# A running logsumexp over 4096 rows: Exp and Ln by column chunks, a carry in two halves, and loads and stores on one queue

## The chip, the cores and the metric

The kernel runs on one core of a Trainium2 chip. A core has a matrix engine (TensorE, PE in the profile, with PEld for its weight loads), a vector engine (VectorE, DVE), an engine for functions such as exp and ln (ScalarE, ACT), a general one (GpSimd, POOL) and one that mostly issues transfers (SyncE, SP). Each engine takes its instructions in order. 16 DMA engines move data between the large memory (HBM) and the on-chip memory (SBUF); PE writes its results to a separate accumulation memory (PSUM).

The metric is device time in microseconds (us), the median over several runs. The times before the change are 1268.48 to 1272.39 us over 8 runs, median 1270.67 us.

## The reference

The input x has the shape (4, 4096, 4128) in float32: 4 batches, 4096 rows that are scanned in order, 4128 independent columns. The output is the running logsumexp along the rows:

```
out[:, 0, :] = x[:, 0, :]
for t in range(1, S):
    mx = maximum(out[:, t-1, :], x[:, t, :])
    out[:, t, :] = mx + log(exp(out[:, t-1, :] - mx) + exp(x[:, t, :] - mx))
```

So out[t] = ln(exp(x[0]) + ... + exp(x[t])). The kernel computes it in that form, without the maximum: Exp of everything, a running sum, Ln of the sums.

## The kernel before, in words

The rows are cut into steps of 256 (P * R = 128 x 2), so there are 4 x 16 = 64 steps, and the running sum passes from each step to the next within a batch. A step's tile `xt` is 128 partitions by 2 rows by 4128 columns of float32: partition p holds the rows 2p and 2p+1 of the step, which lie next to each other in HBM, so that one partition's part is one piece of 33024 bytes. One load (L135) and one store (L126) move the whole tile, 4128 KB each. `xt` has 5 buffers; the results are written back into the same buffer and stored from it, so a buffer is free for another load only when its store has landed.

Exp of the whole tile is one instruction (L139), into a float16 tile `et`. The running sum over the 256 rows is made by matrix products with constant 128 x 128 matrices, in column chunks of 1024 (`CH`), each as two matmuls of 512 (`MM`); every matmul goes through the helper at L80. For the first of the two rows of each partition, `head(c)` adds in one PSUM tile `pt`:

- `incl` times the first rows: all first rows up to and with this partition;
- `excl` times the second rows: all second rows of the partitions before;
- `last` times `carry[c]`: the sum at the end of the step before (left out at the first step of a batch).

Ln (L98) turns that into the output of the first rows. Then `second(c)` adds `ident` times the second rows onto the same PSUM tile, Ln (L105) gives the second rows, and DVE copies the whole PSUM tile to `carry[c]` in float16 (L106). `last` has ones in its last row only, so the next step takes partition 127 of the carry, which holds the total. There are four chunks of 1024 and a tail of 32 columns, which has its own small PSUM tile `qt`, one Ln (L124) and one copy (L125). `pt` has 3 buffers, each of 1024 float32 columns.

The order is written out by hand (`manual_schedule`), and the engines follow it. The loop at L133 issues, for step i+1, the load and Exp, and then the scan of step i: on ACT, Exp of step i+1 stands ahead of all Ln of step i. Loads are on SP's queue. Stores are on GpSimd's (L126), which does nothing else after the constants are built. So two DMA queues feed the same 16 DMA engines: q1 with the loads, q0 with the stores.

Of the kernel before, what the change touches and what calls it, by code (L numbers as in the profile page):

```python
# [1 line left out]

# [4 lines left out]

FP32 = mybir.dt.float32
FP16 = mybir.dt.float16
ACT = mybir.ActivationFunctionType  # L10
P = 128
R = 2
CH = 1024
MM = 512


def _constants(nc, pool):


    def tri(base, name):  # L20
        t = pool.tile([P, P], FP16, name=name)
        nc.gpsimd.memset(t, 1.0)

        nc.gpsimd.affine_select(  # L24
            out=t, in_=t, pattern=[[1, P]], compare_op=mybir.AluOpType.is_ge,
            fill=0.0, base=base, channel_multiplier=-1,
        )
        return t

    def ones_where_zero(base, mult, step, name):  # L30
        t = pool.tile([P, P], FP16, name=name)
        nc.gpsimd.memset(t, 0.0)
        nc.gpsimd.affine_select(  # L33
            out=t, in_=t, pattern=[[step, P]], compare_op=mybir.AluOpType.not_equal,
            fill=1.0, base=base, channel_multiplier=mult,
        )
        return t

    return (
        tri(0, "incl"),  # L40
        tri(-1, "excl"),
        ones_where_zero(0, 1, -1, "ident"),
        ones_where_zero(-(P - 1), 1, 0, "last"),
    )


@with_exitstack
def kernel(
    ctx: ExitStack,
    tc: tile.TileContext,  # L50
    x: bass.AP,
    out: bass.AP,
):

    nc = tc.nc
    B, S, D = x.shape
    rows = P * R
    n_t = S // rows  # L60
    assert S % rows == 0
    n_main = D // CH
    tail = D - n_main * CH
    t0 = n_main * CH

    nc.scalar.preload_act_table_set("natural_log_exp_and_others")  # L66
    consts = ctx.enter_context(tc.tile_pool(name="consts", bufs=1))
    incl, excl, ident, last = _constants(nc, consts)

    xpool = ctx.enter_context(tc.tile_pool(name="xpool", bufs=5))  # L70
    epool = ctx.enter_context(tc.tile_pool(name="epool", bufs=2))
    cpool = ctx.enter_context(tc.tile_pool(name="cpool", bufs=1))
    pmain = ctx.enter_context(tc.tile_pool(name="pmain", bufs=3, space=bass.MemoryType.PSUM))
    ptail = ctx.enter_context(tc.tile_pool(name="ptail", bufs=2, space=bass.MemoryType.PSUM))

    carry = [cpool.tile([P, CH], FP16, name=f"carry{c}") for c in range(n_main)]
    carry_t = cpool.tile([P, tail], FP16, name="carry_t") if tail else None

    def mm(pt, w, rhs, start, stop):
        nc.tensor.matmul(pt, lhsT=w, rhs=rhs, start=start, stop=stop, skip_group_check=True)  # L80

    def scan(b, k, xt, et):
        first = k == 0

        def head(c):
            pt = pmain.tile([P, CH], FP32, name="pt")
            for s in range(0, CH, MM):
                o = pt[:, s:s + MM]
                seg = slice(c * CH + s, c * CH + s + MM)
                mm(o, incl, et[:, 0, seg], True, False)  # L90
            for s in range(0, CH, MM):
                o = pt[:, s:s + MM]
                seg = slice(c * CH + s, c * CH + s + MM)
                mm(o, excl, et[:, 1, seg], False, first)
            if not first:
                for s in range(0, CH, MM):
                    mm(pt[:, s:s + MM], last, carry[c][:, s:s + MM], False, True)
            nc.scalar.activation(xt[:, 0, c * CH:(c + 1) * CH], pt, ACT.Ln)  # L98
            return pt

        def second(c, pt):
            for s in range(0, CH, MM):
                seg = slice(c * CH + s, c * CH + s + MM)
                mm(pt[:, s:s + MM], ident, et[:, 1, seg], False, True)
            nc.scalar.activation(xt[:, 1, c * CH:(c + 1) * CH], pt, ACT.Ln)  # L105
            nc.vector.tensor_copy(carry[c], pt)  # L106

        prev = None
        for c in range(n_main):
            pt = head(c)  # L110
            if prev is not None:
                second(c - 1, prev)
            prev = pt
        if tail:
            qt = ptail.tile([P, R, tail], FP32, name="qt")
            seg = slice(t0, D)
            for j in range(R):
                mm(qt[:, j, :], incl, et[:, 0, seg], j == 0, False)
                mm(qt[:, j, :], incl if j else excl, et[:, 1, seg], False, first)
                if not first:  # L120
                    mm(qt[:, j, :], last, carry_t, False, True)
        second(n_main - 1, prev)
        if tail:
            nc.scalar.activation(xt[:, :, t0:D], qt, ACT.Ln)  # L124
            nc.vector.tensor_copy(carry_t, qt[:, 1, :])  # L125
        nc.gpsimd.dma_start(  # L126
            out=out[b, k * rows:(k + 1) * rows, :].rearrange("(p j) d -> p j d", j=R), in_=xt,
        )

    ctx.enter_context(tc.manual_schedule())  # L130
    work = [(b, k) for b in range(B) for k in range(n_t)]
    pending = None
    for b, k in work:  # L133
        xt = xpool.tile([P, R, D], FP32, name="xt")
        nc.sync.dma_start(  # L135
            out=xt, in_=x[b, k * rows:(k + 1) * rows, :].rearrange("(p j) d -> p j d", j=R),
        )
        et = epool.tile([P, R, D], FP16, name="et")
        nc.scalar.activation(et, xt, ACT.Exp)  # L139
        if pending is not None:  # L140
            scan(*pending)
        pending = (b, k, xt, et)
    scan(*pending)


# [1 line left out]
_INS = ['x']  # L147
_OUTS = [((4, 4096, 4128), 'float32')]


# [23 lines left out]
```

## Time and profile before

| what | value |
|---|---|
| median of 8 runs | 1270.67 us |
| the profiled execution's own time | 1270.67 us |
| its span | 1269.0 us |
| PE busy | 611.2 us, 48% |
| DVE busy | 313.8 us, 25% |
| ACT busy | 948.9 us, 75% |
| Exp (L139), 64 instructions | 453.4 us, 7084 ns each |
| Ln (L98 and L105), 512 instructions | 254.2 and 255.0 us, 1019 and 1027 ns each |
| carry copy (L106), 256 instructions | 307.6 us, 1222 ns each |
| mean granted clock of PE | 0.761 |
| read from HBM, written to HBM | 270.53 MB, 270.53 MB |
| mean rate over the span | 426 GB/s |

Busy time of an engine is the time in which it works on at least one instruction, so neighbours that overlap a little are not counted twice. The profile cuts the span in 40 equal slices of 31.7 us; a row of digits gives an engine's busy share in each in tenths, and the rows DMA and GB/s give the mean busy share of the 16 DMA engines and what they moved. In a list of waits, each line names who waited, the instruction it waited for, the total in us, how many times, and the longest. In a table of stretches, each line has the stretch, its length, and for each engine its busy time and instructions, then the granted clock of PE, the DMA share and the rate; a packet's bytes are counted where it starts, so a share or a rate can pass the limit a little in a short stretch.

### The profile page before, as it was taken

Reading aid. Unit: us, or ns where it says so; the run is one execution under the profiler, and the core shown is the slowest. Engines: PE = TensorE matmul, PEld = TensorE weight load, DVE = VectorE, ACT = ScalarE, POOL = GpSimd, SP = SyncE. Lnnn points to the kernel's source line nnn. Section 1 sums busy time; section 2 is a strip of 40 time slices with the busy share of each in tenths; the row PEclk is TensorE's granted clock in tenths of the full one; section 3 lists DMA queues with packets and bytes.
Section 4 is the critical chain, followed back from the end, with each engine's and each line's share of the span. In section 5 each row is a group of like instructions: output and inputs, shape, how many; then the busy total and the mean of one; then the engine's idle time right before and its main releaser. Section 6 shows DMA issues by size and latency. Waiting matters only on the chain.

```text
span 1269.0 us, 6438 instructions
## 1 busy us (share of the span) xinstructions
PE 611.2 (48%) x2392; PEld 242.6 (19%) x2392; DVE 313.8 (25%) x320; ACT 948.9 (75%) x641; POOL 36.0 (3%) x76
## 2 busy tenths in 40 slices
PE   1565355354454454544535445454453554544543
PEld 0222122121121221211212112121121221211211
DVE  0332122231231222312223122132231222312213
ACT  5887777777777777677776777777777777677774
POOL 0000000000000000000000000000000000000000
PEclk9787787786777867778768687786877877768777
DMA  9999999999999999999999999999999999999996
GB/s 401 424 420 433 434 433 434 432 433 433 432 433 432 432 433 433 433 433 433 433 433 433 433 432 433 433 433 433 432 433 433 433 432 433 432 434 433 433 407 271
DMA packets 18463, 541.47 MB, mean 427 GB/s; under 512 B 2048, under 2 KB 2048, under 8 KB 2048
## 3 DMA queue, kind: packets, MB, share of 16 engines
q1 hardware_dynamic: 9216, 270.54, 49.6%
q0 software_dynamic: 9216, 270.54, 49.5%
q8 instruction: 18, 0.29, 0.1%
q14 instruction: 13, 0.11, 0.0%
HBM read 270.53 MB, written 270.53 MB: 426 GB/s over the span
## 4 chain that ended last, share of the span: by engine, by line
issue 89%; DMA 6%; POOL 2%; ACT 1%; PE 0%; DVE 0%; POOLq 0%; DVEq 0%; SPq 0%
DMA xt<-in_x_dram 3%; DMA out_dram<-xt 3%; POOL out_dram L126 2%; PE pt L80 0%; ACT xt L98 0%; ACT xt L105 0%; DVE carry L106 0%; POOLq L126 0%; DVEq L169 0%; DVE carry_t L125 0%; ACT et L139 0%; SPq L135 0%; DVEq L125 0%
## 5 line engine op out<-in xcount | busy, mean ns | idle before, releaser
L139 ACT ACTIVATE et<-xt 128x8256 f16<-128x8256 f32 x64 | 453.4, 7084 | 178.5 <-DMA xt<-in_x_dram 178.5
L106 DVE CAST carry<-pt 128x1024 f16<-128x1024 f32 x256 | 307.6, 1222 | 940.9 <-ACT xt L105 940.9
L80 PE MATMUL pt<-et,ident 128*128 128x512 f16 x512 | 198.9, 479 | 599.8 <-ACT xt L98 599.8
L98 ACT ACTIVATE xt<-pt 128x1024 f32<-128x1024 f32 x256 | 254.2, 1019 | 113.4 <-PE pt L80 112.7
L105 ACT ACTIVATE xt<-pt 128x1024 f32<-128x1024 f32 x256 | 255.0, 1027 | 11.7 <-PE pt L80 11.7
L80 PE MATMUL pt<-et,incl 128*128 128x512 f16 x512 | 194.2, 468 | 40.9 <-DVE carry L106 20.5
L80 PE MATMUL pt<-et,excl 128*128 128x512 f16 x512 | 187.5, 454 | 0.0
L80 PEld LDWEIGHTS <-ident 128*128 128x128 f16 x512 | 56.0, 109 | 680.2 <-issue 656.8
L80 PE MATMUL pt<-carry,last 128*128 128x512 f16 x480 | 167.5, 436 | 0.0
L80 PEld LDWEIGHTS <-incl 128*128 128x128 f16 x704 | 74.2, 112 | 153.2 <-issue 116.6
L80 PEld LDWEIGHTS <-excl 128*128 128x128 f16 x576 | 65.0, 113 | 97.5 <-issue 51.6
L80 PEld LDWEIGHTS <-last 128*128 128x128 f16 x600 | 63.6, 108 | 78.0 <-issue 37.2
L126 POOL DMA_DIRECT2D out_dram<-xt x64 | 34.2, 534 | 1217.4 <-ACT xt L124 1217.4
L80 PE MATMUL qt<-et,incl 128*128 128x32 f16 x192 | 17.9, 178 | 0.0
L124 ACT ACTIVATE xt<-qt 128x64 f32<-128x64 f32 x64 | 16.2, 253 | 0.0
L80 PE MATMUL qt<-carry_t,last 128*128 128x32 f16 x120 | 15.1, 176 | 0.0
L125 DVE CAST carry_t<-qt 128x32 f16<-128x32 f32 x64 | 11.6, 181 | 0.0
L80 PE MATMUL qt<-et,excl 128*128 128x32 f16 x64 | 11.3, 177 | 0.0
L66 ACT ACT_TABLE_LOAD x1 | 1.3, 1283 | 0.8 <-PEq L158 0.8
L24 POOL TENSOR_SCALAR_AFFINE_SELECT incl<-incl 128x128 f16<-128x128 f16 x1 | 0.3, 287 | 0.0
L24 POOL TENSOR_SCALAR_AFFINE_SELECT excl<-excl 128x128 f16<-128x128 f16 x1 | 0.3, 286 | 0.0
L33 POOL TENSOR_SCALAR_AFFINE_SELECT ident<-ident 128x128 f16<-128x128 f16 x1 | 0.3, 286 | 0.0
(9 smaller groups left out, 1.5 us busy)
## 6 DMA issues: line engine op xcount, KB each, us to landing
xt<-in_x_dram SPq DMA_DIRECT2D x64, 4128.0 KB, 27.0
out_dram<-xt POOLq DMA_DIRECT2D x64, 4128.0 KB, 34.2
```

Source lines behind the costliest of these rows:

```text
L24: nc.gpsimd.affine_select(out=t, in_=t, pattern=[[1, P]], compare_op=mybir.AluOpType.is_ge, fill=0.0, base=base, channel_multiplier=-1,)
L33: nc.gpsimd.affine_select(out=t, in_=t, pattern=[[step, P]], compare_op=mybir.AluOpType.not_equal, fill=1.0, base=base, channel_multiplier ...
L66: nc.scalar.preload_act_table_set("natural_log_exp_and_others")
L80: nc.tensor.matmul(pt, lhsT=w, rhs=rhs, start=start, stop=stop, skip_group_check=True)
L98: nc.scalar.activation(xt[:, 0, c * CH:(c + 1) * CH], pt, ACT.Ln)
L105: nc.scalar.activation(xt[:, 1, c * CH:(c + 1) * CH], pt, ACT.Ln)
L106: nc.vector.tensor_copy(carry[c], pt)
L124: nc.scalar.activation(xt[:, :, t0:D], qt, ACT.Ln)
L125: nc.vector.tensor_copy(carry_t, qt[:, 1, :])
L126: nc.gpsimd.dma_start(out=out[b, k * rows:(k + 1) * rows, :].rearrange("(p j) d -> p j d", j=R), in_=xt,)
L139: nc.scalar.activation(et, xt, ACT.Exp)
```

## The change

The matrices stay, and so do the bytes moved, the buffers of `xt` (5) and of PSUM (3 and 2). What changes:

- Exp is done by column chunk: three instructions of 2 x 1024 and one of 2 x 1056 elements per partition, each into its own `et` tile (4 buffers of one chunk in place of 2 of a whole step). The tail's columns are in the last chunk's tile.
- A step is no longer spread over two turns of the loop. Within a step, ACT's order is Exp 0, Exp 1, Ln of chunk 0's first rows, Exp 2, Ln of chunk 1's first rows, Ln of chunk 0's second rows, Exp 3, and so on. PE's order is written so that `head(c)` and, for the last chunk, the tail's matmuls stand ahead of `second(c-1)`.
- The carry is kept in two halves. DVE copies partitions 96 to 127 of PSUM to float16 (`HI`), and writes the difference between PSUM and that copy to partitions 32 to 63 (`LO`). `pick` replaces `last`, with ones in the rows 127 and 63, so that the matmul adds the rounded total and what the rounding left. The carry tiles are set to zero once.
- Loads and stores are both on SP's queue. The load of step i+3 is issued ahead of step i's work, its store after it, so that the queue has four loads, and then a store and a load by turns: L0 L1 L2 L3 S0 L4 S1 L5 S2 and so on. In the end come S59 L63 S60 S61 S62 S63.

```diff
+HI, LO = 96, 32
...
-        ones_where_zero(-(P - 1), 1, 0, "last"),
+        ones_where_zero([-(HI + 31), -(LO + 31)], 0, "pick"),
...
-    epool = ctx.enter_context(tc.tile_pool(name="epool", bufs=2))
+    epool = ctx.enter_context(tc.tile_pool(name="epool", bufs=4))
...
+    for t in (*carry, carry_t):
+        nc.vector.memset(t, 0.0)
...
+    def keep(cr, pt):
+
+        nc.vector.tensor_copy(cr[HI:HI + 32, :], pt[HI:HI + 32])
+        nc.vector.tensor_tensor(
+            out=cr[LO:LO + 32, :], in0=pt[HI:HI + 32], in1=cr[HI:HI + 32, :],
+            op=mybir.AluOpType.subtract,
+        )
+
+    class Step:
+        def __init__(self, b, k):
+            self.first = k == 0
+            self.xt = xpool.tile([P, R, D], FP32, name="xt")
...
+            nc.sync.dma_start(out=self.xt, in_=self.dram(x))
...
+        def exp(self, c):
+            s = self.cols(c)
+            w = s.stop - s.start
+            et = epool.tile([P, R, CH + tail], FP16, name="et")
+            nc.scalar.activation(et[:, :, :w], self.xt[:, :, s], ACT.Exp)
+            self.et[c] = et
...
+        def close(self, c):
+
+            self.ln(1, c)
+            keep(carry[c], self.pt[c])
...
+        def store(self):
+            nc.sync.dma_start(out=self.dram(out), in_=self.xt)
+
+        def run(self):
+            last = n_main - 1
+            self.exp(0)
+            self.head(0)
+            for c in range(1, n_main):
+                self.exp(c)
+                self.head(c)
+                if c == last:
+                    self.tail_mm()
+                self.ln(0, c - 1)
+                self.second(c - 1)
+                if c >= 2:
+                    self.close(c - 2)
+            self.ln(0, last)
+            self.second(last)
+            self.close(last - 1)
+            self.ln_tail()
+            self.close(last)
+            self.store()
...
-        nc.gpsimd.dma_start(
-            out=out[b, k * rows:(k + 1) * rows, :].rearrange("(p j) d -> p j d", j=R), in_=xt,
-        )
...
+    ahead = 3
+    steps = []
+    for i, (b, k) in enumerate(work):
+        if i == 0:
+            steps += [Step(*work[n]) for n in range(ahead)]
+        if i + ahead < len(work):
+            n = i + ahead
+            steps.append(Step(*work[n]))
+        steps[i].run()
```

## The prediction

> **What bounds the kernel now.** I read the page's engine shares first, then its forty slices, then the waits, then stretches with one kind of transfer in flight.
>
> ```profile
> span 1269.0 us, 6438 instructions
> PE 611.2 (48%) x2392; PEld 242.6 (19%) x2392; DVE 313.8 (25%) x320; ACT 948.9 (75%) x641; POOL 36.0 (3%) x76
> ...
> DMA  9999999999999999999999999999999999999996
> GB/s 401 424 420 433 434 433 434 432 433 433 432 433 432 432 433 433 433 433 433 433 433 433 433 432 433 433 433 433 432 433 433 433 432 433 432 434 433 433 407 271
> ...
> q1 hardware_dynamic: 9216, 270.54, 49.6%
> q0 software_dynamic: 9216, 270.54, 49.5%
> ```
>
> ACT, the busiest compute engine, works 948.9 / 64 = 14.8 us of each of the 64 steps. The 16 DMA engines are full in 39 of 40 slices, at 433 GB/s. A transfer is 128 x 8256 x 4 B = 4.227 MB, so 4.227 / 433 = 9.76 us, and a load and a store 19.52 us: the step. DMA is the bound; only the first three and last two slices fall short of 433.
>
> ```profile
> ACT et L139 <- DMA xt<-in_x_dram: 178.5, 61, 11.1
> ...
> SPq L135 <- DMA out_dram<-xt: 1175.1, 59, 59.8
> ```
>
> Both waits (waits of the engines; waits of SP's own queue) say it again: ACT waits for a load at 61 of 64 steps, and SP waits before each load for a store to free the buffer. Now the ends. The columns of the first fence are busy time of PE, PEld, DVE, ACT, POOL, then PE clock, DMA share, GB/s.
>
> ```profile
> 0.00:1.00 1.00, 0.00 (x0) 0.00 (x0) 0.00 (x0) 0.19 (x1) 0.40 (x6) 1.00 0.00 0
> 1.00:2.00 1.00, 0.00 (x0) 0.10 (x1) 0.00 (x0) 1.00 (x1) 0.96 (x7) 1.00 1.37 363
> 5.00:35.00 30.00, 7.34 (x18) 2.54 (x18) 1.23 (x1) 18.22 (x7) 0.00 (x0) 0.86 1.00 434
> 600.00:700.00 100.00, 46.44 (x180) 18.47 (x180) 24.51 (x25) 75.81 (x51) 2.66 (x5) 0.72 1.00 433
> 1235.00:1243.00 8.00, 6.71 (x30) 2.79 (x30) 2.66 (x3) 6.55 (x8) 0.00 (x0) 0.78 0.22 95
> 1243.00:1244.00 1.00, 0.78 (x4) 0.26 (x3) 1.00 (x2) 0.93 (x3) 0.00 (x0) 1.00 0.00 0
> 1244.00:1245.00 1.00, 0.93 (x5) 0.45 (x5) 1.00 (x2) 0.89 (x1) 0.53 (x1) 1.00 0.04 8
> 1245.00:1264.00 19.00, 5.30 (x29) 2.19 (x27) 5.14 (x7) 6.74 (x8) 0.53 (x1) 0.78 1.04 445
> 1264.00:1265.00 1.00, 0.00 (x0) 0.00 (x0) 0.00 (x0) 0.00 (x0) 0.00 (x0) 0.50 0.00 0
> ```
>
> ```profile
> 13.22 7.08 ACT L139 ACTIVATE et<-xt 128x8256 f16<-128x8256 f32 x1 [11.13 <-DMA xt<-in_x_dram]
> 22.99 7.08 ACT L139 ACTIVATE et<-xt 128x8256 f16<-128x8256 f32 x1 [2.69 <-DMA xt<-in_x_dram]
> ...
> 1225.62 0.53 POOL L126 DMA_DIRECT2D out_dram<-xt  x1 [19.54 <-ACT xt L124]
> 1227.61 7.08 ACT L139 ACTIVATE et<-xt 128x8256 f16<-128x8256 f32 x1 [2.28 <-DMA xt<-in_x_dram]
> 1244.09 0.53 POOL L126 DMA_DIRECT2D out_dram<-xt  x1 [17.94 <-ACT xt L124]
> 1253.57 0.53 POOL L126 DMA_DIRECT2D out_dram<-xt  x1 [8.95 <-ACT xt L124]
> ```
>
> The last load lands at 1227.6; then Exp and the scan of step 62 run 16.5 us before its store can be issued (1244.09). Store 61 (1225.62) drains meanwhile, and from 1235 to 1245 the DMA engines are nearly empty: 8 x 0.78 + 1 + 0.96 = 8.2 us. Then stores 62 and 63 run alone, done by about 1264.8, and the span ends 4.2 us later.
>
> **The change, part by part.**
>
> Bytes: unchanged. Sum of before by this account: first byte 1.4 (the rows of 0 to 2 us), 128 x 9.76 = 1249.3, 4.2 at the end: 1254.9. The span is 1269.0, so 14.1 us are lost to DMA gaps and slow packets: 8.2 in the hole; the rest in the first slices ((433-401)+(433-424)+(433-420) = 54 GB/s over 31.7 us slices, 4.0 us, less the 1.4 counted, 2.6), the last two stores, and small losses between.
>
> The hole at the end goes. SP's order becomes L0 L1 L2 L3 S0 L4 S1 L5 ... S59 L63 S60 S61 S62 S63. Store 59 enters the queue before load 63, so behind load 63 lie stores 60 to 63, 4 x 9.76 = 39 us of transfers, while step 63 needs one step time, worked out next at 15 to 18.2 us. Gain 8.2 us.
>
> The step's compute must stay under 19.52. ACT: one Exp of 8256 elements (7084 ns) becomes three of 2048 and one of 2112. The rows of 8256 (7084) and 1024 (1019) elements give 0.839 ns per element and 160 ns fixed: 3 x 1.88 + 1.93 = 7.57, 0.5 more. Eight Ln, 4 x 1.019 + 4 x 1.027 = 8.18, tail 0.25: 16.0. Neighbours overlap in the trace (before: durations add to 15.52, busy is 14.83, 0.08 at each of 9 joints); with 13 joints 15.0. PE does the same 32 large matmuls. At granted clock 0.50 (the trace has pairs 0.86 us apart) a head of six takes 2.6 us, while ACT has 1.9 us of other work (an Exp, or two Ln): 0.7 to 0.8 late, at four heads at most 3.2. So a step is 15.0 to 18.2 us. It is 1.3 us or more below the DMA's 19.52, and costs nothing. If that cover is gone, each us above 19.52 costs 64 us.
>
> DVE: a 128x1024 copy (1222 ns) becomes a 32-partition copy and a subtract of the same length, neither shown. Bounds for each: a quarter of 1222 if partitions counted, or 1222 if only the row's length does; I take 1222, since 128x32 costs 181 and the length sets it. Per step 8 x 1.22 + 4 x 0.18 is at most 10.5 us. PE waits for it before reusing one of three PSUM buffers: Ln of the second row, then 2 x 1.22 = 2.44 on DVE, against the 1.9 us Exp in between: 0.5 late at most, inside the 0.8 above when the clock is low. Hidden. The five memsets and one more affine_select (0.29 us) run before load 0 lands at 13.2: nothing.
>
> Waits on SP. Each store now waits on SP for its last Ln, and load i+4 is queued behind it; load i+5 also waits until store i has landed. Nothing else is on SP. Between store i and load i+5 the queue holds load i+4 and store i+1, 19.5 us of transfers, against a landing of at most 4.2 us (last byte to the span's end) and an issue to first byte of 0.6 (0.81 to 1.4): covered. At the start, load 0 lands at 13.2, store 0 is issued by 13.2 + 18.2 = 31.4, and loads 0 to 3 last until about 41: covered by 10 us. POOL issued the stores and nothing else; 34 us of issue goes there, worth nothing.
>
> The rate of the one queue is the open price. Loads behind loads in SP's queue land 22.99 - 13.22 = 9.77 apart, 434 GB/s in 5 to 35: passing from one load to the next costs nothing. In 600 to 700 the engines take loads and stores by turns from two queues at 433: changing direction costs nothing either. Stores alone in one queue: 1.04 x 19 = 19.8 us for two, 9.9 each. A load behind a store in the same queue is not shown. So a store costs 9.76 to 9.9 us; I take 9.82, the middle, since its neighbours are loads but it runs in a block as those two did. Load 0 lands at 13.22, which is 2.05 after 1.4 + 9.77: slow start and landing delay together. Between 0 and 2.05 I charge 0.7 of it to the DMA engines. Of the 2.6 lost in the first slices that leaves 1.9, where the first stores begin; it may come back, but I take none of it and keep it for the range.
>
> The Trainium skill, "DMA: Bandwidth & Descriptors", in its anatomy of one DMA, speaks against it: about 2 us of fixed cost per transfer, mostly the wait for the write receipt, longest towards HBM. If a following transfer of the same queue waited for that, 64 stores would cost 128 us more, 1385 by that rule. The two stores above, 9.9 apiece, deny it on the other queue; no row has it on SP's.
>
> Sum: 1.4 + 0.7 + 64 x (9.76 + 9.82) + 4.2 = 1259.4 span. The profiled execution took 1270.67 for its 1269.0 span, 1.67 outside, and equals the median of the runs. Forecast 1261.1, say **1261 us**, -0.8%. With stores at 9.76: 1257; at 9.9 and the 1.9: 1268. Own range 1255 to 1268.
>
> **The rivals.**
>
> A, slower: the one queue loses time whenever it passes between a store and a load. Place: each DMA engine's ring, 128 passages. Price per passage: from 0 (the rows above) to a full issue-to-first-byte, 0.6 to 0.8 us (load 0.81 to 1.4; store 1244.09 to about 1244.9). It decides at (1273.2 - 1257) / 128 = 0.13 us. At 0.3 us: 1257 + 38 = 1295; at 0.7, 1347. For: queue 1 never carried both kinds, and two queues can hide each other's gaps. Against: neither a change of direction nor a following transfer showed one.
>
> B, no change: stores in blocks cost slightly more than 9.9, say 9.95 with small passage losses, and eat the hole's gain: 1257 + 64 x 0.19 = 1269. For: the lone stores are the nearest row. Against: the page's mixed rows.
>
> C, slower: the interleaved chain ACT-PE-ACT-DVE takes over, at 20.5 us a step: 13.2 to the first landing, 64 x 20.5 = 1312, a last store of 9.8, 4.2 and 1.7: 1341. For: PE must wait for ACT and DVE several times a step. Against: needs 2.3 us above the half-clock sum of 18.2.
>
> D, the change doesn't act: stores in order behind loads still leave step 63 as a tail. It would need step times above 39 us; 1270. Hardly possible.
>
> **How the numbers follow.** Forecast 0.68, A 0.16, B 0.10, C 0.05, D 0.01. 0.2% of 1270.67 is 2.5 us, about what a measurement of this kernel can tell from no change: bounds 1268.1 and 1273.2. Faster: 0.68 and a little of B, 0.70; same: most of B and D, 0.09; slower: A and C, 0.21. The range takes in forecast, B and the cheap part of A (to 0.2 us a passage, 1257 + 26 = 1283): 1254 to 1284.
>
> **What would show it.** Right: GB/s 430 or more in every slice but the last, no empty stretch in the last 40 us, a store always on SP's queue ahead of need, ACT waiting for loads at most steps with Exp rows near 1.9 us, span near 1259. Wrong: GB/s evenly below 428 with DMA share under 1 (A or B); DMA share falling with ACT or PE waiting on each other and loads landed long before (C); a hole after load 63 (D).

## The result and the profile after

The changed kernel takes 1265.07 us (median of 12 runs, 1264.69 to 1266.5) beside 1270.76 us for the kernel before: a ratio of 0.9949 with a 95% interval of 0.9936 to 0.9963. It is faster by half a per cent; 1261 was forecast, with its own range from 1255 to 1268. Kernels that use two DMA queues had some much longer executions; a ratio leaves out those more than 1.5% above the shortest of their kernel, and one profile below, of the stores on GpSimd, is of a longer execution (1285.6 us).

The profiled execution of the changed kernel took 1266.5 us, the longest of the twelve, with a span of 1264.6. Its page has, against the lines shown of before:

```profile
span 1264.6 us, 7025 instructions
PE 660.5 (52%) x2392; PEld 241.6 (19%) x2392; DVE 655.7 (52%) x645; ACT 962.3 (76%) x833; POOL 2.2 (0%) x13
...
GB/s 401 412 430 432 435 431 425 430 431 432 424 432 433 433 433 432 433 430 431 434 434 433 429 434 433 433 434 432 429 431 435 435 434 430 431 435 433 434 435 329
...
q1 hardware_dynamic: 18432, 541.07, 99.5%
```

All bytes are now on one queue, DVE works twice as long, and the rate is still about 433 GB/s in most slices. DMA still bounds the kernel. The waits of the engines say the same as before: ACT waits for a load at 55 of 64 steps.

```profile
PE pt L86 <- DVE carry L91: 162.9, 64, 2.9
ACT et L111 <- DMA xt<-in_x_dram: 153.1, 55, 11.1
ACT xt L126 <- PE pt L86: 64.5, 66, 1.8
```

And in the waits of SP's own queue, it mostly waits for a store to land before it may issue a load:

```profile
SPq L102 <- DMA out_dram<-xt: 1079.9, 59, 19.1
SPq L153 <- ACT xt L126: 89.9, 9, 16.9
```

The difference is at the end. The timeline of ACT there, and that of SP's queue:

```profile
1224.48 3.71 ACT L111 ACTIVATE et<-xt 128x2048 f16<-128x2048 f32 x2 [3.06 <-DMA xt<-in_x_dram]
...
1240.32 1.04 ACT L126 ACTIVATE xt<-pt 128x1024 f32<-128x1024 f32 x1
```

```profile
1195.48 46.25 SPq L153 DMA_DIRECT2D out_dram<-xt  x4
```

The last load lands at 1224.5. Stores 60 to 63 are issued from 1195.5 on, the last by 1195.48 + 46.25 = 1241.7. So the last step's work, 16.9 us on ACT, lies wholly beside stores that are already queued. In the table of stretches (busy time of PE, PEld, DVE, ACT, POOL, then clock, DMA share, GB/s) the old hole is gone:

```profile
0.00:100.00 100.00, 51.99 (x181) 18.79 (x182) 50.69 (x54) 77.96 (x68) 2.16 (x13) 0.84 0.99 415
100.00:300.00 200.00, 112.79 (x418) 41.79 (x417) 110.86 (x108) 162.48 (x142) 0.00 (x0) 0.80 1.00 430
500.00:700.00 200.00, 107.26 (x381) 39.09 (x381) 102.14 (x100) 154.13 (x134) 0.00 (x0) 0.75 1.00 433
...
1240.00:1250.00 10.00, 0.06 (x1) 0.00 (x0) 5.40 (x7) 1.37 (x3) 0.00 (x0) 0.63 1.04 450
1250.00:1260.00 10.00, 0.00 (x0) 0.00 (x0) 0.00 (x0) 0.00 (x0) 0.00 (x0) 0.50 0.69 297
1260.00:1261.00 1.00, 0.00 (x0) 0.00 (x0) 0.00 (x0) 0.00 (x0) 0.00 (x0) 0.50 0.08 33
1261.00:1262.00 1.00, 0.00 (x0) 0.00 (x0) 0.00 (x0) 0.00 (x0) 0.00 (x0) 0.50 0.00 0
1262.00:1263.00 1.00, 0.00 (x0) 0.00 (x0) 0.00 (x0) 0.00 (x0) 0.00 (x0) 0.50 0.08 33
```

But part of the old loss is still there, at another place. From 1250 on the share falls to 0.69 and then to 0.08: at 1260 and at 1262 a single packet of 33 KB starts, so one DMA engine of 16 is still at work. A transfer is 128 pieces of 33 KB, 8 for each engine. In the trace's packet records, which have the start and end of each piece (one packet), the 16 engines end the last store between 1254.6 and 1263.3 us, 8.7 us apart, and the last one sets the time.

The row of GB/s gives the whole account. A slice's loss is (433 - its rate) / 433 times its length, 31.7 us before and 31.6 after:

| loss against 433 GB/s, us | before | after |
|---|---|---|
| slices 1 to 3 | 4.0 | 4.1 |
| slices 4 to 11 | 0.0 | 1.8 |
| slices 12 to 38 | 0.4 | 0.8 |
| slices 39 and 40 | 13.8 | 7.4 |
| sum | 18.1 | 14.1 |
| span less the sum | 1250.9 | 1250.5 |

By these averages the end gains 6.4 us, and slower slices between 95 and 350 us and small losses later take 2.2 us of it back. But an average over 16 engines hides which engine sets the time. In the packet records of the kernel before, the engines end store 61 between 1236.6 and 1243.1 us, and from 1238.1 on one of them works alone. All 16 are idle only from 1243.1 to 1245.2, when store 62 begins, and they end store 62 within 0.3 us of each other. So of the hole of 8.2 us, 2.0 was lost to the last engine; the rest was early engines that waited for it and for the store. The engines were unequal before too, and the hole let the late ones catch up.

In the changed kernel no moment between the first byte and the last has all engines idle. The last byte is at 1263.3, and the span ends 1.3 us later; before, with the stores on GpSimd, the last byte was at 1265.1 and the span ended 3.8 us later. (The prediction's 4.2, and the 1.7 in the expectations below, come from the stretches, with the first byte at 1.4; by the packet records it is at 1.8. The difference of 2.5 us is the same.) The 2.0 us of the idle engines and these 2.5 us make 4.5; the spans differ by 4.4.

### The profile page after: what moved, and what is told of

Same layout as the page of the kernel before. It is cut to its first block, busy times and chain, and to the rows that moved or that the text cites. A ratio compares the mean times of both kernels' runs of the same rounds, so it can differ in the third digit from the quotient of the medians.

```text
span 1264.6 us, 7025 instructions
## 1 busy us (share of the span) xinstructions
PE 660.5 (52%) x2392; PEld 241.6 (19%) x2392; DVE 655.7 (52%) x645; ACT 962.3 (76%) x833; POOL 2.2 (0%) x13
## 4 chain that ended last, share of the span: by engine, by line
DMA 81%; ACT 2%; issue 1%; DVE 1%; SPq 1%; PE 1%; ACTq 0%
DMA out_dram<-xt 74%; DMA xt<-in_x_dram 7%; ACT et L111 1%; ACT xt L126 1%; SPq L102 1%; PE pt L86 1%; DVE carry L90 0%; DVE carry L91 0%; SPq L153 0%; DVE carry_t L90 0%; DVE carry_t L91 0%; ACTq L126 0%
## 5 line engine op out<-in xcount | busy, mean ns | idle before, releaser
L90 DVE CAST carry<-pt 32x1024 f16<-32x1024 f32 x256 | 314.8, 1230 | 575.9 <-ACT xt L126 572.9
L111 ACT ACTIVATE et<-xt 128x2048 f16<-128x2048 f32 (+1 forms) x256 | 485.5, 1921 | 153.1 <-DMA xt<-in_x_dram 153.1
L126 ACT ACTIVATE xt<-pt 128x1024 f32<-128x1024 f32 x512 | 504.3, 1028 | 125.2 <-PE pt L86 64.5
L86 PE MATMUL pt<-et,incl 128*128 128x512 f16 x512 | 211.6, 506 | 552.2 <-ACT et L111 388.9
L91 DVE TENSOR_TENSOR carry<-pt,carry 32x1024 f16<-32x1024 f32 x256 | 314.0, 1226 | 8.9
L86 PE MATMUL pt<-et,excl 128*128 128x512 f16 x512 | 210.3, 503 | 0.0
L86 PE MATMUL pt<-carry,pick 128*128 128x512 f16 x480 | 194.1, 496 | 0.0
L86 PE MATMUL pt<-et,ident 128*128 128x512 f16 x512 | 173.2, 424 | 27.3 <-ACT xt L126 27.3
L86 PEld LDWEIGHTS <-pick 128*128 128x128 f16 x600 | 69.2, 117 | 93.8 <-issue 64.7
L86 PE MATMUL qt<-carry_t,pick 128*128 128x32 f16 x120 | 15.6, 182 | 0.0
L90 DVE CAST carry_t<-qt 32x32 f16<-32x32 f32 x64 | 12.6, 197 | 2.0
```

The source lines that it names most:

```text
L90: nc.vector.tensor_copy(cr[HI:HI + 32, :], pt[HI:HI + 32])
L91: nc.vector.tensor_tensor(out=cr[LO:LO + 32, :], in0=pt[HI:HI + 32], in1=cr[HI:HI + 32, :], op=mybir.AluOpType.subtract,)
L111: nc.scalar.activation(et[:, :, :w], self.xt[:, :, s], ACT.Exp)
L126: nc.scalar.activation(self.xt[:, j, c * CH:(c + 1) * CH], self.pt[c], ACT.Ln)
```

## The experiments

Two theories stood against each other. Theory Q: the one queue brings the gain, since four stores lie behind the last load. Theory I: the interleaved order of Exp and Ln brings it. The first two kernels do one part each. In them "one queue" always takes with it the order of its transfers, with loads three steps ahead.

**Stores on GpSimd again, all else as changed.**

```diff
-            nc.sync.dma_start(out=self.dram(out), in_=self.xt)
+            nc.gpsimd.dma_start(out=self.dram(out), in_=self.xt)
```

> The changed kernel with one edit: the store is issued from GpSimd, so loads and stores are on two queues again; Exp, Ln and the carry stay interleaved. Theory Q (the gain comes from the one queue, in which four stores lie behind the last load): with two queues the last store can be issued only after the last load has landed and one step of 15 to 18 us has passed, while at that time little more than one store is left to drain, so an empty stretch of 5 to 8 us comes back before the last store, and 4.2 us after the last byte in place of the 1.7 of the changed kernel: 1269 to 1273 us. Theory I (the gain comes from the interleaved order): 1264 to 1267 us, no empty stretch.

Measured: a ratio to the kernel before of 1.0052 (1.0015 to 1.009), with executions from 1268.83 to 1366.02 us. The gain is gone: none of the twelve comes near 1265. The lines are of the 1285.6 us execution, first its stretches, then POOL's timeline:

```profile
100.00:300.00 200.00, 108.52 (x384) 39.38 (x383) 103.72 (x102) 151.34 (x131) 5.33 (x10) 0.75 1.00 423
...
1245.00:1255.00 10.00, 3.65 (x10) 1.28 (x10) 6.21 (x7) 5.87 (x6) 0.53 (x1) 0.66 0.92 396
1255.00:1265.00 10.00, 6.33 (x28) 2.47 (x27) 4.32 (x4) 8.07 (x7) 0.00 (x0) 0.83 0.49 211
```

```profile
1247.19 0.53 POOL L153 DMA_DIRECT2D out_dram<-xt  x1 [19.30 <-ACT xt L126]
1268.42 0.53 POOL L153 DMA_DIRECT2D out_dram<-xt  x1 [20.70 <-ACT xt L126]
```

The last two stores are 21 us apart, one drains in 10, and the half-empty stretch is back (0.49 from 1255 to 1265). Theory Q foresaw that stretch. But by the packet records it costs this execution nothing: the engines end store 62 between 1258.2 and 1270.3 us, and the last of them goes on to store 63 at once and ends it at 1280.1, 9.8 us later. The time is lost elsewhere: 14.9 us by the GB/s row in slices 4 to 38, where theory Q did not foresee 423 GB/s, and 3.8 us after the last byte. Why the shortest executions take 1269 us is not shown, since this profile is of a longer one.

**The old order on one queue.** Exp of a whole step, Exp ahead of the Ln of the step before, one carry copy; only the queue and the time of the loads are those of the changed kernel.

```diff
-        nc.gpsimd.dma_start(
+        nc.sync.dma_start(
...
+    for n in range(3):
+        load(n)
     for i, (b, k) in enumerate(work):
+        if 1 <= i and i + 2 < len(work):
+            load(i + 2)
+        xt = tiles[i]
```

> The kernel before with one edit: the stores go to SP's queue, and the loads are issued in the order of the changed kernel (L0 L1 L2 L3 S0 L4 S1 ... S59 L63 S60 to S63). Exp stays one instruction of 8256 elements, Exp of step i+1 stays ahead of the Ln of step i, and the carry is one copy. Theory Q: behind the last load lie the same four stores, 39 us, and the last step's store is ready 16.5 + 9.5 = 26 us after the last load, so no empty stretch: 1263 to 1267 us, the same as the changed kernel. Theory I: 1269 to 1272 us, as the kernel before.

Measured: 1263.29 us (1262.15 to 1263.82), ratio 0.9938 (0.9926 to 0.995). The queue, with its loads three ahead, brings the whole gain, and 1.8 us more than the full change, so the interleaved order is not needed for it. 2.6 us of it are the time after the last byte, 1.2 in place of 3.8. One point of theory Q's expectation was wrong; the stretches, ACT's timeline and SP's, one after another, show it:

```profile
1230.00:1240.00 10.00, 8.86 (x34) 3.46 (x34) 3.95 (x4) 7.54 (x10) 0.00 (x0) 0.72 0.59 254
1240.00:1250.00 10.00, 6.01 (x32) 2.55 (x30) 5.42 (x6) 7.34 (x9) 0.00 (x0) 0.96 1.00 427
```

```profile
1222.27 7.08 ACT L150 ACTIVATE et<-xt 128x8256 f16<-128x8256 f32 x1 [2.75 <-DMA xt<-in_x_dram]
...
1239.26 0.24 ACT L124 ACTIVATE xt<-qt 128x64 f32<-128x64 f32 x1
...
1248.74 0.24 ACT L124 ACTIVATE xt<-qt 128x64 f32<-128x64 f32 x1
```

```profile
1199.66 49.67 SPq L126 DMA_DIRECT2D out_dram<-xt  x4
```

There is an empty stretch of 4.1 us (0.41 of 10). In this order Exp of step 63 stands ahead of the Ln of step 62, so store 62 is ready only at 1239.5, 17 us after the last load landed, and store 63 at 1199.66 + 49.67 = 1249.3. It costs little, because the late DMA engines use it to catch up: by the packet records the 16 engines end store 61 between 1233.3 and 1241.3 us, and store 62 and the last store within 0.9 us, where the changed kernel had 8.7. The hole and the unequal ends stand in for one another, and at no moment are all engines idle.

**Transfers alone, on one queue and on two.** No Exp, matmuls, Ln or carry; the tile is stored as loaded.

```diff
         def run(self):
-            last = n_main - 1
-            self.exp(0)
...
             self.store()
```

> The changed kernel without Exp, matmuls, Ln and carry: each step's tile is loaded and stored again, in the same order on SP's queue, so the output is the input. It shows what the 128 transfers of one queue cost by themselves. If passing from a store to a load on one queue costs nothing and the 5 us of unequal ends of the DMA engines in the changed kernel come from instruction fetches, which this kernel has hardly any of: 1.4 + 128 x 9.76 + 1.7 is a span of 1252.4, with slow start 1253 to 1255, so 1254 to 1257 us, and all DMA engines end within 2 us. If the ends are unequal for another reason (queue, HBM): 1260 to 1265 us, and unequal ends again.

> The same without computation, the stores on GpSimd's queue. If the two queues take turns at no loss: 1.4 + 1249.3 + 4.2 is a span of 1255, 1256 to 1259 us. If one queue is slower by itself (passage loss hidden by two queues), this kernel is clearly faster than the transfers on one queue; if the queue of GpSimd costs extra, slower by more than the 2.5 us at its end.

Measured: one queue 1261.1 us (1260.08 to 1261.52), ratio 0.992 (0.9907 to 0.9933); two queues 1259.01 us, ratio 0.9905 (0.9891 to 0.992), with one of the four executions at 1294.64 us. So computation adds only 4 us to the transfers of the changed kernel. In these stretches the columns are DVE, ACT, POOL, clock, DMA share, GB/s; first one queue, then two:

```profile
100.00:300.00 200.00, 0.00 (x0) 0.00 (x0) 0.00 (x0) 1.00 1.00 431
500.00:700.00 200.00, 0.00 (x0) 0.00 (x0) 0.00 (x0) 1.00 1.00 433
...
1250.00:1260.00 10.00, 0.00 (x0) 0.00 (x0) 0.00 (x0) 1.00 0.40 172
```

```profile
100.00:300.00 200.00, 0.00 (x0) 0.00 (x0) 5.32 (x10) 1.00 1.00 433
...
1250.00:1252.00 2.00, 0.00 (x0) 0.00 (x0) 0.00 (x0) 1.00 0.84 363
1252.00:1257.00 5.00, 0.00 (x0) 0.00 (x0) 0.00 (x0) 1.00 0.03 13
```

Both run at 433 GB/s in 500 to 700: passing between a store and a load on one queue costs nothing there. But the one queue is slower in 100 to 300, and leaves its engines 6.2 us apart at the end (two queues: 1.4). The page shows one instruction packet here against 34 in the changed kernel, so my guess that instruction fetches set the engines apart falls. In the packet records the longer packets of the one queue are nearly all of loads (142 of 144 over 1.26 us, where the usual is 1.22), 112 of them in the first 330 us; why, stays open.

**Half transfers.** Loads and stores alone, on one queue, moved as first rows and second rows by turns.

```diff
+        for j in range(R):
+            if n < len(work):
+                steps[n].load(j)
+            steps[i].save(j)
```

> Loads and stores alone, without computation (the output is the input), on SP's queue, but each tile is moved in two halves, first rows and second rows, so that half loads and half stores take turns (16.5 KB pieces in place of 33 KB). With whole tiles one queue took 1261.1 us and two queues 1259.0, and the slow packets of the one queue were nearly all in loads of the first 330 us, which left the DMA engines 6 us apart at the end. If the length of a block of one kind makes the slow packets: 1256 to 1259 us and engines closer together. If a transfer's end costs something in itself, twice as many ends cost more: 1264 us or above. If neither: 1260 to 1262 us.

Measured: 1266.83 us (1266.68 to 1267.96), ratio 0.9967 (0.9955 to 0.998), and 430 to 431 GB/s throughout. Shorter blocks do not help. With 128 more transfer ends, and pieces half as long, 5.7 us are added to the 1261.1 of whole tiles, 0.045 us for each end. The Trainium skill's "DMA: Bandwidth & Descriptors", in its anatomy of one DMA, gives some 2 us per transfer for the GpSimd path, mostly the write receipt, and calls it completion latency. This case agrees with a latency: as a price for the next transfer of SP's queue, which stays filled, the measurement is some forty times less.

**One half of the carry.** The subtract is left out, and the second half of the carry stays zero.

```diff
         nc.vector.tensor_copy(cr[HI:HI + 32, :], pt[HI:HI + 32])
-        nc.vector.tensor_tensor(
-            out=cr[LO:LO + 32, :], in0=pt[HI:HI + 32], in1=cr[HI:HI + 32, :],
-            op=mybir.AluOpType.subtract,
-        )
```

> The changed kernel, one queue, without the subtract: only the rounded half of the carry is kept (the other half of the carry tile stays zero), so the carry is as exact as in the kernel before. DVE loses 4 x 1.23 us a step. If the second half of the carry is hidden, as the prediction had it: 1263.5 to 1266.5 us, within 0.1% of the changed kernel's 1265.07. If it is what makes the changed kernel slower than the old order on one queue (1263.29): 1262 to 1263.5 us.

Measured: 1263.0 us (1262.62 to 1263.4), ratio 0.9934 (0.9919 to 0.9949). This is the old order's 1263.29 again: on one queue interleaving brings nothing, and the second half of the carry costs 2 us, though the loads still set the pace. These kernels were timed on different chips, but the kernel before beside them agrees within 0.3 us (1270.68 and 1270.96). The next two kernels, on a third chip, say which part of it costs.

**The changed kernel again, and its subtract with the result put elsewhere.**

```diff
+    scr = cpool.tile([P, CH], FP16, name="scr")
...
-            out=cr[LO:LO + 32, :], in0=pt[HI:HI + 32], in1=cr[HI:HI + 32, :],
+            out=scr[LO:LO + 32, :cr.shape[-1]], in0=pt[HI:HI + 32], in1=cr[HI:HI + 32, :],
```

> The changed kernel as it is, on the same chip and beside the two next kernels: 1264.5 to 1266.5 us if the 2 us between it and the kernel with the single carry are real, since those two were timed in different jobs.

> The changed kernel with DVE's subtract kept, same size and operands, but written to a tile that nothing reads; the second half of the carry stays zero, as in the kernel with the single carry (1263.0). If the 2 us of the second half come from DVE's added work itself (its reads of PSUM, its hold on a PSUM buffer, its traffic beside the transfers): 1264.5 to 1266.5 us, as the changed kernel. If they come from PE's wait for the second half of the carry or from its nonzero data: 1262.5 to 1263.5 us.

Measured: 1265.09 us (1264.36 to 1265.64) and 1265.49 us (1264.87 to 1265.73). So the 2 us come with DVE's work itself (its reads, its hold on a PSUM buffer and its writes are not told apart), not from PE's wait for the second half or from its data. The single carry was not timed beside these two, so the 2 us rest on the changed kernel's own agreement, 1265.07 us first and 1265.09 here. By the GB/s rows the single carry loses 10.3 us, the changed kernel in this second profile 12.8 and this kernel 13.2; most of the difference lies in the last slice (5.8, 7.3 and 7.8). The stretch from 1250 us, for the three in this order, shows how much is still to be moved there:

```profile
1250.00:1264.00 14.00, 0.00 (x0) 0.00 (x0) 0.00 (x0) 0.00 (x0) 0.00 (x0) 0.54 0.37 161
1250.00:1264.00 14.00, 0.00 (x0) 0.00 (x0) 0.00 (x0) 0.00 (x0) 0.00 (x0) 0.50 0.42 179
1250.00:1264.00 14.00, 0.00 (x0) 0.00 (x0) 0.00 (x0) 0.00 (x0) 0.00 (x0) 0.50 0.43 186
```

By the packet records the engines end 7.3, 8.9 and 9.7 us apart, further when DVE works more. What DVE does to a DMA engine was not tried.

**Stores on ACT, and stores on GpSimd with a single carry.** The first has two hardware queues, the second the DVE work of before.

```diff
-            nc.sync.dma_start(out=self.dram(out), in_=self.xt)
+            nc.scalar.dma_start(out=self.dram(out), in_=self.xt)
```

> The changed kernel with the stores issued from ACT: two hardware queues, no GpSimd. Theory Q (order behind the last load decides): the last store again comes about 17 us after the last load, while the other queue has little left, so an empty stretch of 5 to 8 us comes back: 1268 to 1272 us. If instead the loss of the stores on GpSimd was that queue's own (its 4.2 us after the last byte, its slow packets in the steady part), two hardware queues give 1264 to 1267 us. The steady part tells too: 433 GB/s if the slow packets of the run with GpSimd belong to that queue, 423 to 429 if they belong to any two queues.

> Stores on GpSimd and only the rounded half of the carry, so DVE works as much as in the kernel before. The run with stores on GpSimd moved only 423 to 429 GB/s in its steady part, and its executions scattered from 1268.8 to 1366. If DVE's doubled work slows the transfers of GpSimd's queue, both are gone here: 433 GB/s and 1268 to 1272 us, the empty stretch at the end remaining. If the interleaved order or two queues as such do it: scatter and 423 to 429 GB/s again.

Measured: 0.9981 (0.9952 to 1.0011), nine of the 12 executions between 1265.75 and 1266.59 and three from 1282 to 1357; and 0.9995 (0.9964 to 1.0027), from 1266.7 to 1325.88. Neither ratio is told apart from the kernel before, but longer executions raise both. The nine of stores on ACT lie 4.4 to 5.2 us below the kernel before beside them (1270.96) and some 1.2 us above the changed kernel, in the range expected if the loss was the GpSimd queue's own. So one queue is not the only way to most of the gain: two hardware queues with the interleaved order have it too, in these nine executions.

The profile of the single carry on GpSimd is of a short one (1269.24 us), and its hole is small:

```profile
1240.00:1250.00 10.00, 5.91 (x29) 2.24 (x26) 3.70 (x4) 9.71 (x10) 0.00 (x0) 0.94 0.73 315
```

By its packet records the last engine ends store 62 at 1254.0 us and store 63 at 1263.8, without a pause, and the span ends 3.8 us later. So with the interleaved order the hole costs the last engine nothing in this execution, even on two queues. Theory I holds for that part on two queues; with one queue the order isn't needed.

The single carry on GpSimd runs at 431 to 432 GB/s in its steady part, so the 423 of the first run is not there, but the long executions are: DVE's work doesn't explain them, and neither does GpSimd's queue, since the two hardware queues have them too, nor the computation, since transfers alone on two queues had one (1294.64). The five kernels that move whole tiles on SP's queue with loads three ahead (the changed one twice) each kept their own repetitions within 2 us.

**One step ahead.**

```diff
-    ahead = 3
+    ahead = 1
```

> The changed kernel with loads one step ahead in place of three, so the queue is L0 L1 S0 L2 S1 L3 ... L63 S62 S63: behind the last load lie two stores, not four. The prediction said that cover is what hides a step. Behind load i+1 only store i and load i+2 lie, 19.5 us against a step of 15 to 18 us and the landing: the steady part should just hold or lose up to 1 us a step, and behind the last load store 62 has 9.8 us against 17: an empty stretch of about 8 us. 1272 to 1340 us. If the depth did not matter: 1265.

Measured: 1329.5 us, ratio 1.0456 (1.0429 to 1.0483). The depth of the queue is worth 64 us. SP's wait, in the waits of its queue, has changed sides, from stores to ACT, and the rate falls in the steady stretches:

```profile
SPq L153 <- ACT xt L126: 1097.1, 64, 17.9
SPq L153 <- DMA xt<-in_x_dram: 159.7, 62, 11.4
```

```profile
500.00:700.00 200.00, 104.41 (x358) 37.46 (x358) 98.31 (x98) 147.44 (x126) 0.00 (x0) 0.74 1.00 415
```

The empty stretch at the end came as expected: by the packet records all engines are idle for 9.2 us from 1306.2 on, before the last store (and for 6.8 us near the start, from 22.5 on). In the steady part the expectation, up to 1 us a step lost to empty queues, has the right size and not the right form: the share stays near 1, and pieces take longer. After 100 us some 900 of the 1000 pieces over 1.35 us begin 9 to 12 us after a store was issued, about where that store ends and the load behind it begins. Why this passage costs time here, and none with loads three ahead, was not found.

## Why the prediction was right, and where it was off

**The bound and the cover: right. The worth of the hole: too large.** DMA stays the bound, and the four stores behind the last load cover the last step: no moment has all engines idle. The old order on one queue shows that the queue does it, and the depth of one, with 9.2 us of idle engines, that the cover is needed on one queue. But the 8.2 us were worked out from the mean share of 16 engines. On the last engine the hole was 2.0 us; the rest came back as unequal ends.

**Costed at nothing: stores leaving GpSimd.** The prediction kept 4.2 us after the last byte, and called the move away from POOL worth nothing. It was worth 2.5 us, more than the hole on the last engine. This gain was not foreseen and made up for a part of the 6.2 us by which the hole was over-valued, so that the time falls inside the range is in part luck. Stores on ACT, with most of the gain on two queues, point the same way.

**The step's compute: right.** ACT's busy time is 962.3 / 64 = 15.04 us a step where 15.0 was worked out. The groups of the changed kernel:

```profile
L90 DVE CAST carry<-pt 32x1024 f16<-32x1024 f32 x256 | 314.8, 1230 | 575.9 <-ACT xt L126 572.9
L111 ACT ACTIVATE et<-xt 128x2048 f16<-128x2048 f32 (+1 forms) x256 | 485.5, 1921 | 153.1 <-DMA xt<-in_x_dram 153.1
...
L91 DVE TENSOR_TENSOR carry<-pt,carry 32x1024 f16<-32x1024 f32 x256 | 314.0, 1226 | 8.9
```

A copy of 32 partitions takes as long as one of 128 (1230 ns against 1222), so the row's length sets it. DVE has 655.7 / 64 = 10.2 us a step, 10.5 at most was said. PE waits for it once a step, 162.9 / 64 = 2.5 us where 0.5 at most was said, and ACT for PE 64.5 us in all; both are hidden, since ACT still ends up waiting for loads.

**Costed at nothing, and wrong by 2 us: the second half of the carry.** Its cover, the wait for loads, holds; with it the transfers end 2 us later, and how DVE's work does that is open.

**The rate of the one queue: the size was off, the middle was right.** I charged each store 0.06 us more than a load, 3.8 in all. In the steady part nothing is lost (433 GB/s from 500 to 700). Slices 4 to 39 lose 2.4 us, most of it before 350 us. So the sign "430 or more in every slice but the last" failed, in six slices (401 to 429). Rival A, a loss at each passage, does not happen with loads three ahead: its price is at most the 0.045 us of a transfer's end, against 0.13 where it would decide.

**Mis-sized: the start.** Slices 1 to 3 lose 4.1 us where I charged 1.4 + 0.7. The 1.9 us where the first stores begin, which I left for the range, came back in full; in the second profile of the changed kernel (1264.88 us) these slices lose 3.4, so part of it varies.

**Mis-sized: the end.** I charged 4.2 us for it. The time after the last byte is 1.3, but the last slice loses 7.6, since the 16 DMA engines don't end together. What is late at the end is not the last store's issue but the slowest engine. In the kernel before, this was hidden in the hole.

These terms, as averages over the engines, together: 1259.4 was the span forecast; the start adds 2.0, the end 3.4, the steady part takes 1.4 off (2.4 for 3.8), and the span less its losses is 1250.5 where 128 x 9.76 gave 1249.3, 1.2 more. That is 1264.6, the span of the profiled execution.

**One queue or two.** The Trainium skill's "DMA: Bandwidth & Descriptors", under issuing engines, says that these are not separate DMA queues: all share the same 16 engines, and issuing from several only saves issue time. The steady rates agree (433 on one queue and on two). The whole time does not follow from it: in the old order one queue in place of two brought 7 us, 2.6 of them after the last byte.

## What to carry to other kernels

When the DMA engines are full nearly everywhere, look at the two ends of the profile: the time still to be had is where they run dry. But a mean share over the engines is not time: a stretch at 0.22 can be one late engine at work and 15 that wait, so look for the moments when all are idle, and at the last engine. Loads and stores on one in-order queue, loads a few steps ahead, leave a reserve of stores behind the last load; check that this reserve is longer than a step's latency, as the one-step depth shows. Look too at what comes after the last byte, which here depended on the queue of the last store. Work that is hidden behind transfers is not always free, so test it by taking it away alone.

## What the runs showed that was not expected

- The DMA engines drift apart: 8.7 us by the end of the changed kernel, 6.5 at store 61 of the kernel before, 6.2 with transfers alone on one queue, 1.4 on two. A transfer's landing is that of the slowest.
- Interleaved kernels with two queues had executions from 1266 to 1366 us, whichever engine issued the stores, and transfers alone on two queues had one 35 us above the rest. The kernels with one queue didn't. The cause was not found.
- With loads one step ahead the DMA share stays at 0.98 to 1.00 while the rate falls to 412 to 417 GB/s: a packet then takes longer, and the busy share hides it.
- With the last store on SP's queue or on ACT's the span ended 1.2 to 1.3 us after the last byte; from GpSimd it was 3.8.
